# A two-layer hybrid trunk: the loads of the modulation's weights are issued from GpSimd's queue

## The chip, the cores and the metric

The kernel runs on one core of one Trainium2 chip. The metric is the device time of one execution in microseconds (us). The core has five engines with a queue of instructions each: PE (TensorE, the matmuls; PEld is its weight loads), DVE (VectorE), ACT (ScalarE), POOL (GpSimd) and SP (SyncE). Each works through its own queue in order and waits on semaphores for the others. A transfer is issued by an instruction in one engine's queue and carried out by 16 DMA engines.

## The reference, cut to what matters

Two layers of a trunk, each with four groups of heads (latent attention, banded attention, gated delta rule, long convolution) and an MLP, for 128 context and 1024 latent tokens, width 1024, all in float32. The lines that the change touches are those of the modulation:

```python
def trunk_layer(x, cond, P, mixer):
    mod = jnp.einsum('bd,de->be', jax.nn.silu(cond), P['w_ada']) + P['b_ada']
    sh1, sc1, gt1, sh2, sc2, gt2 = jnp.split(mod[:, None, :], 6, axis=-1)
    h = rms_norm(x, P['g_pre_mix']) * (1.0 + sc1) + sh1
    o, extra = mixer(h)
    x = x + gt1 * rms_norm(o, P['g_post_mix'])
    h = rms_norm(x, P['g_pre_mlp']) * (1.0 + sc2) + sh2
    m = jnp.einsum('blf,fd->bld', jnp.square(jax.nn.relu(jnp.einsum('bld,df->blf', h, P['mlp_w1']))), P['mlp_w2'])
    x = x + gt2 * rms_norm(m, P['g_post_mlp'])
```

`w_ada` is 1024 x 6144 in each layer, 24 MB. It depends on nothing but the two conditions (`c` and `c_ctx`), so it may be multiplied long before its result is used.

## The kernel before

All of the kernel is one class, `Trunk`. The modulation is worked out by `ada(l, g)` (line 384), a Python generator, in six groups: layer `l` 0 or 1, and `g` 0 to 2, a third of the columns each (the first two sections, the next two, the last two of the six). One group loads 32 tiles `wada` of 128 x 512 float32 (256 KB; 8 slices `kt` of the contracted width by 4 column blocks `h`) and multiplies each with the conditions into one PSUM tile `ada`; the four matmuls of a `kt` write the four 32-row quarters of it. Then ACT copies the tile out (`adarow`, line 398), PE transposes it (`adat`) and DVE adds the bias (`mod`, line 406).

The tiles `wada` come from the pool of tag `T`, which has four buffers. So a load may be issued only when the matmul that used the buffer four loads earlier is done. Loads of other weights (`wa`, `wb`, `w`) take buffers of the same tag in other stages. Before the change every DMA of the kernel, these loads too, is issued from SP's queue.

`layer(l)` (its caller) runs three generators in turn by a virtual clock, `run_timed((rest(), 1.5), (ahead(other()), GD), (adas(), 1))`. `rest` is the projections, the preparation of the latent attention, the convolution (`hyena`) and the attention; `other` is the delta rule's preparation and scan (`gdn_scan`), at a higher priority; `adas` waits until the projections are done and then steps through `ada` for the groups (l,1), (l,2) and (l+1,0). The group (0,0) runs by itself at the program's start. So in layer 0 three groups (96 loads) run beside the scan, the convolution and the beginning of the attention, and in layer 1 two (64 loads).

The order in which these generators emit is not yet the order of the engines: the program is built under `tile.TileContext(nc, schedule_with_timeline_sim=True)`, whose scheduler orders each engine's instructions by times that it works out for itself. A changed instruction can thus move others on every engine.

Names used below. In `gdn_scan`: `u`, `dS` and `St` are the matmuls and the state of a step, `sc` and `Q` hold its output (lines 1388, 1389), which goes to the DRAM tensor `goscr` (line 1392); after the last step `o` is loaded from `goscr` (line 1413), POOL adds both directions (line 1417), ACT and DVE normalise it and PE transposes it (`oT`). In `hyena`: POOL makes `pm`, `sd` and `ZA` (line 1465) and the two halves of `Y` (lines 1605, 1606); PE transforms (`X`, `iz`). In the attention: `K`, `Q`, `VA` are loaded (lines 752 to 759), `S` are the scores, `mx` their maxima.

Of the kernel before, what the change touches and what calls it, by code (L numbers as in the profile page):

```python
# [158 lines left out]
def bc(ap, n):  # L159

    return ap.unsqueeze(len(ap.shape)).broadcast_to(list(ap.shape) + [n])


class Trunk:
# [220 lines left out]
    def ada(self, l, g, tag="T"):  # L385

        nc = self.nc
        ps = self.P(name="ada")
        for kt in range(8):
            for h in range(4):  # L390
                w = self.H(name="wada", tag=tag[h % len(tag)])
                i = nc.sync.dma_start(out=w, in_=self.I["w_ada"][l, kt, :, g * 2048 + h * 512:g * 2048 + (h + 1) * 512])
                self.mm(ps[32 * h:32 * h + 32, :], self.cst[:, kt], w, kt == 0, kt == 7)
            if l == g == 0:
                self.lead = i
            yield
        row = self.H(name="adarow")
        nc.scalar.copy(out=row, in_=ps)
        pt = self.P((4, 2, 2, 32), name="adat")
        for b in range(4):  # L400
            self.tr(pt[:, b], row[:, b * 128:(b + 1) * 128])

        for half in range(2):
            o = self.mod[l][:, g, half * 4:half * 4 + 4]
            b = self.bada[l].rearrange("p (g s h b) -> p g s h b", g=3, s=2, h=2)[:, g, :, half].rearrange("p s b -> p b s")
            nc.vector.tensor_tensor(out=o, in0=pt[:, :, :, half, 0:2], in1=bc(b, 2), op=ALU.add)
        yield
# [1841 lines left out]
```

## Time and profile before

| | us |
|---|---|
| median of 3 runs | 3819.6 |
| lowest, highest | 3818.95, 3856.05 |
| the profiled execution | 3818.92 |
| its span in the trace | 3817.1 |
| PE busy in the span | 3530.3 |
| DVE busy | 2236.0 |
| ACT busy | 1367.0 |
| POOL busy | 710.1 |

The profile is of one execution. Busy time is what an engine spends in its operations; issues of DMAs, semaphores and branches are not counted in it. A row of the timeline is one group of like instructions in a line: its start, its length, what it did, how many (x), and in brackets how long the engine had been idle before it and what released it. `SPq` is an issue in SP's queue. `DMA` in a window is the mean busy share of the 16 DMA engines, `PEclk` the clock that was granted to PE, 1 being full.

### The profile page before, as it was taken

Reading aid. Unit: us, or ns where it says so; the run is one execution under the profiler, and the core shown is the slowest. Engines: PE = TensorE matmul, PEld = TensorE weight load, DVE = VectorE, ACT = ScalarE, POOL = GpSimd, SP = SyncE. Lnnn points to the kernel's source line nnn. Section 1 sums busy time; section 2 is a strip of 40 time slices with the busy share of each in tenths; the row PEclk is TensorE's granted clock in tenths of the full one; section 3 lists DMA queues with packets and bytes.
Section 4 is the critical chain, followed back from the end, with each engine's and each line's share of the span. In section 5 each row is a group of like instructions: output and inputs, shape, how many; then the busy total and the mean of one; then the engine's idle time right before and its main releaser. Section 6 shows DMA issues by size and latency. Waiting matters only on the chain. (4 is left out here: it accounts for less than half of the span.)

```text
span 3817.1 us, 58820 instructions
## 1 busy us (share of the span) xinstructions
PE 3530.3 (92%) x22478; PEld 2940.8 (77%) x22478; DVE 2236.0 (59%) x4583; ACT 1367.0 (36%) x2972; POOL 710.1 (19%) x710
## 2 busy tenths in 40 slices
PE   7989888799899999999989798787989999999998
PEld 4879774366689999999968787545656899999997
DVE  5765567677645444444586674767774544444446
ACT  5434343265543122212364334323664422222112
POOL 1152531013420000000131633211143200000003
PEclk9998889799999999999999898897989999999999
DMA  5346476832421111111334465755414211111113
GB/s 203 115 115 158 137 266 201 240 84 60 141 86 48 42 45 44 35 44 45 100 104 129 112 151 151 262 185 167 101 40 138 72 45 45 45 45 45 39 39 122
DMA packets 364677, 405.40 MB, mean 106 GB/s; under 512 B 115816, under 2 KB 237158, under 8 KB 364395
## 3 DMA queue, kind: packets, MB, share of 16 engines
q1 hardware_dynamic: 364394, 401.63, 35.1%
q8 instruction: 177, 2.90, 0.3%
q14 instruction: 106, 0.86, 0.1%
HBM read 298.34 MB, written 103.19 MB: 105 GB/s over the span
## 5 line engine op out<-in xcount | busy, mean ns | idle before, releaser
L213 PE MATMUL hid<-hT,w1h 128*128 128x384 f32 x3072 | 786.6, 335 | 0.1
L213 PE MATMUL pj<-hT,wah 128*128 128x384 f32 x2112 | 575.8, 351 | 10.4 <-ACT wah L253 4.2
L1839 DVE TENSOR_TENSOR acc<-acc,mo 128x512 f32<-128x512 f32 x504 | 345.9, 686 | 391.9 <-PE mo L213 391.9
L213 PEld LDWEIGHTS hid<-hT,w1h 128*128 128x128 f32 x3072 | 557.6, 188 | 14.4 <-ACT h L481 1.1
L213 PE MATMUL hid<-hT,w1l 128*128 128x384 f32 x1536 | 514.1, 335 | 0.0
L213 PE MATMUL mo<-w2h,ul 128*128 128x512 f32 x1116 | 435.0, 392 | 0.0
L213 PE MATMUL mo<-w2h,uh 128*128 128x512 f32 x1080 | 422.7, 391 | 0.0
L213 PE MATMUL mo<-w2l,uh 128*128 128x512 f32 x1080 | 422.7, 391 | 0.0
L213 PEld LDWEIGHTS pj<-hT,wah 128*128 128x128 f32 x2112 | 396.3, 196 | 23.3 <-issue 7.5
L213 PE MATMUL pj<-hT,wal 128*128 128x384 f32 x1056 | 368.2, 349 | 0.7 <-DVE wal L232 0.7
L242 ACT CAST w2h<-w 128x512 fp32r<-128x512 f32 x128 | 70.3, 619 | 732.7 <-PE mo L213 728.5
L269 POOL TENSOR_TENSOR postr<-postr,mhalf 128x1 f32<-128x1 f32 x36 | 22.3, 622 | 1564.1 <-DVE postr L268 1563.7
L213 PEld LDWEIGHTS hid<-hT,w1l 128*128 128x128 f32 x1536 | 288.3, 188 | 2.5
L213 PEld LDWEIGHTS mo<-w2h,ul 128*128 128x128 f32 x1116 | 209.6, 188 | 46.1
L662 POOL TENSOR_TENSOR e<-e,e 128x512 f32<-128x512 f32 (+1 forms) x120 | 162.2, 1353 | 445.3 <-ACT e L651 267.4
L213 PEld LDWEIGHTS mo<-w2h,uh 128*128 128x128 f32 x1080 | 202.8, 188 | 37.5
L213 PEld LDWEIGHTS mo<-w2l,uh 128*128 128x128 f32 x1080 | 202.7, 188 | 36.5
L232 DVE TENSOR_TENSOR el<-e,eh 128x512 fp32r<-128x512 f32 (+1 forms) x252 | 202.3, 820 | 32.2 <-ACT eh L653 30.3
L213 PEld LDWEIGHTS pj<-hT,wal 128*128 128x128 f32 x1056 | 206.4, 195 | 4.6 <-issue 2.0
L1822 DVE SCALAR_TENSOR_TENSOR relu<-hid,relu 128x384 f32<-128x384 f32 x180 | 99.4, 553 | 167.2 <-ACT relu L1821 167.2
L213 PE MATMUL ada<-wada,cst 128*32 128x512 f32 x384 | 137.0, 688 | 46.9 <-DMA wada<-in_w_ada 46.7
L1821 ACT ACTIVATE relu<-hid 128x384 f32<-128x384 f32 x180 | 87.8, 488 | 184.8 <-PE hid L213 184.8
(502 smaller groups left out, 6318.1 us busy)
## 6 DMA issues: line engine op xcount, KB each, us to landing
w<-in_w SPq DMA_DIRECT2D x256, 256.0 KB
wada<-in_w_ada SPq DMA_DIRECT2D x192, 256.0 KB
wa<-in_wa SPq DMA_DIRECT2D x88, 256.0 KB
x<-xres SPq DMA_DIRECT2D x21, 512.0 KB
x<-in_x SPq DMA_DIRECT2D x18, 512.0 KB
Q<-rscr SPq DMA_DIRECT2D x32, 288.0 KB
o<-oscr SPq DMA_DIRECT2D x18, 512.0 KB
xres<-x SPq DMA_DIRECT2D x36, 256.0 KB
```

Of the source, the lines that this page charges most:

```text
L213: self.last = self.nc.tensor.matmul(out, l, r, start=start, stop=stop, skip_group_check=True)
L232: self.nc.vector.tensor_tensor(out=lo, in0=x, in1=hi.bitcast(F32), op=ALU.subtract)
L242: self.nc.scalar.copy(out=hi[:, q], in_=st)
L269: self.nc.gpsimd.tensor_tensor(out=out, in0=out, in1=self.bcs(self.mhalf[:out.shape[0]], out.shape), op=ALU.pow)
L662: self.nc.gpsimd.tensor_tensor(out=acc, in0=acc, in1=e, op=ALU.add)
L1821: nc.scalar.activation(out=r[:, :n], in_=ps[:, :n], func=AF.Relu)
L1822: nc.vector.scalar_tensor_tensor(out=r[:, :n], in0=ps[:, :n], scalar=0.0, in1=r[:, :n], op0=ALU.max, op1=ALU.mult)
L1839: nc.vector.tensor_tensor(out=acc[t][:, ns], in0=acc[t][:, ns], in1=ps, op=ALU.add)
```

## The change

One line of `ada`: all loads but those of the group (0,0) are issued from GpSimd's (POOL's) queue. The order of `T`'s buffers, the transfers and the matmuls stay the same in number.

```diff
@@ ada
         for kt in range(8):
             for h in range(4):
                 w = self.H(name="wada", tag=tag[h % len(tag)])
-                i = nc.sync.dma_start(out=w, in_=self.I["w_ada"][l, kt, :, g * 2048 + h * 512:g * 2048 + (h + 1) * 512])
+                i = (nc.gpsimd if g or l else nc.sync).dma_start(out=w, in_=self.I["w_ada"][l, kt, :, g * 2048 + h * 512:g * 2048 + (h + 1) * 512])
                 self.mm(ps[32 * h:32 * h + 32, :], self.cst[:, kt], w, kt == 0, kt == 7)
```

SP's order has 1566 rows before and 1400 now (like rows in a line are joined), POOL's 701 and 861.

The order of the engines at three places. First POOL in layer 0, at the beginning of the convolution's transforms, before:

```order
L535 TENSOR_TENSOR rsh_6277<-rsh_6277,rS_6276 128x512
L1465 TENSOR_TENSOR pm_6473<-v_6296,v_6298 128x512
L1465 TENSOR_TENSOR sd_6474<-v_6296,v_6298 128x512
L1465 TENSOR_TENSOR ZA_6476<-pm_6473,sd_6474 128x512
L1605 TENSOR_TENSOR Y_6601<-pw_6597 128x256
L1606 TENSOR_TENSOR Y_6601<-pw_6597 128x256
L1605 TENSOR_TENSOR Y_6601<-pw_6609 128x256
L1606 TENSOR_TENSOR Y_6601<-pw_6609 128x256
```

and now:

```order
L392 DMA wada_6402<-in_w_ada 128x512
L535 TENSOR_TENSOR rsh_6277<-rsh_6277,rS_6276 128x512
L1465 TENSOR_TENSOR pm_6473<-v_6296,v_6298 128x512
L1465 TENSOR_TENSOR sd_6474<-v_6296,v_6298 128x512
L1465 TENSOR_TENSOR ZA_6476<-pm_6473,sd_6474 128x512
L1605 TENSOR_TENSOR Y_6601<-pw_6597 128x256
L392 DMA wada_6502<-in_w_ada 128x512
L392 DMA wada_6505<-in_w_ada 128x512
L392 DMA wada_6508<-in_w_ada 128x512
L1606 TENSOR_TENSOR Y_6601<-pw_6597 128x256
L1605 TENSOR_TENSOR Y_6601<-pw_6609 128x256
```

Loads of `wada` now stand between `rsh` (the rope of the attention) and `pm`, and between the two halves of the first `Y`.

Then PE in layer 1 after the last step of the scan, before:

```order
L213 MATMUL ada_24334<-wada_24700,cst 32x512
L213 MATMUL ada_24334<-wada_24703,cst 32x512
L213 MATMUL ada_24334<-wada_24706,cst 32x512
L213 MATMUL ada_24334<-wada_24709,cst 32x512
L229 MATMUL oT_24318<-ident,o_24287 128x128 x4
L229 MATMUL oT_24324<-ident,o_24287 128x128 x4
L229 MATMUL oT_24330<-ident,o_24287 128x128
L229 MATMUL adat_24714<-ident,adarow_24712 128x128 x4
L213 MATMUL S_24727<-K_24629,Q_24627 128x384
L213 MATMUL S_24730<-K_24629,Q_24627 128x384
```

and now:

```order
L213 MATMUL ada_24334<-wada_24700,cst 32x512
L213 MATMUL ada_24334<-wada_24703,cst 32x512
L213 MATMUL ada_24334<-wada_24706,cst 32x512
L213 MATMUL ada_24334<-wada_24709,cst 32x512
L229 MATMUL adat_24714<-ident,adarow_24712 128x128 x4
L213 MATMUL S_24727<-K_24629,Q_24627 128x384
L213 MATMUL S_24730<-K_24629,Q_24627 128x384
L213 MATMUL S_24733<-K_24629,Q_24627 128x384
L213 MATMUL S_24733<-Q_24627 128x128
L213 MATMUL S_24737<-K_24629,Q_24627 128x384
```

The transposes `oT` of the scan's output no longer stand between the last `ada` and `adat`; the scores `S` follow in a run.

At the same place SP's order before, four loads of `wada` stood behind the last `goscr` and the loads of `o`, `Q` and `VA`, and four more behind `x`, `gzl`, `K` and `Q`. Now `K`, `Q` and `VA` for the first scores stand ahead of the last `goscr`, and loads of the output projection's weights (`wo`) between those of `o`.

Last PE in layer 1 earlier in the scan, between its sixth and its seventh step of 18 (`pj` are matmuls of the projections), before:

```order
L213 MATMUL dS_22819<-u_22814,sc_22362 64x64 x2
L213 MATMUL dS_22819<-u_22814,kt_22213 64x64 x2
L213 MATMUL dS_22825<-u_22814,sc_22362 64x64 x2
L213 MATMUL dS_22825<-u_22814,kt_22215 64x64 x2
L213 MATMUL pj_23218<-hT_11158,wah_23208 128x384
L213 MATMUL pj_23218<-hT_11157,wal_23210 128x384
L213 MATMUL pj_23218<-hT_11159,wah_23208 128x384
L213 MATMUL pj_23218<-hT_11160,wah_23208 128x384
L213 MATMUL pj_23218<-hT_11159,wal_23210 128x384
L213 MATMUL pj_23218<-hT_11161,wah_23208 128x384
```

and now:

```order
L213 MATMUL u_22797<-u_22814,Q_20957 64x64
L213 MATMUL u_22797<-u_22814,Q_20974 64x64
L213 MATMUL dS_22825<-u_22814,sc_22362 64x64 x2
L213 MATMUL dS_22825<-u_22814,kt_22215 64x64 x2
L213 MATMUL u_22977<-St_3909_22219,sc_22725 64x64
L213 MATMUL u_22978<-St_3909_22219,sc_22725 64x64
L213 MATMUL u_22977<-St_3909_22219,sc_22725 64x64
L213 MATMUL u_22978<-St_3909_22219,sc_22725 64x64
L213 MATMUL u_22977<-St_3909_22219,WT_21834 64x64
```

Before, 19 `pj` matmuls of 128 x 384 stood between the two steps, and more inside the next. Now the seventh step follows the sixth at once; the fifth to the eighth follow each other with little or nothing of other work between, and the `pj` matmuls stand elsewhere.

## Rows read from the trace of the kernel before

**Rows 1.** Page, part 1: busy us, share of the span, instructions of each engine.

```profile
PE 3530.3 (92%) x22478; PEld 2940.8 (77%) x22478; DVE 2236.0 (59%) x4583; ACT 1367.0 (36%) x2972; POOL 710.1 (19%) x710
```

**Rows 2.** Windows: length, busy us (count) PE PEld DVE ACT POOL, PEclk, DMA, GB/s.

```profile
538.00:768.00 230.00, 187.12 (x1440) 100.62 (x1438) 158.40 (x460) 65.30 (x200) 39.05 (x40) 0.87 0.77 239
...
2454.00:2598.00 144.00, 110.10 (x916) 57.11 (x916) 94.74 (x304) 36.75 (x124) 29.82 (x33) 0.89 0.67 213
```

**Rows 3.** Windows of 40 us, the same columns.

```profile
540.00:580.00 40.00, 26.83 (x301) 17.87 (x298) 34.25 (x106) 14.13 (x48) 16.16 (x18) 0.81 0.93 324
...
700.00:740.00 40.00, 29.60 (x136) 14.77 (x135) 22.36 (x57) 10.89 (x19) 2.62 (x1) 0.76 0.98 285
```

**Rows 4.** PE's waits, 538 to 768 us: waiting line, releaser; total us, times, longest.

```profile
PE ada L213 <- DMA wada<-in_w_ada: 15.0, 12, 4.2
PE X L213 <- DVE ZA L1461: 10.7, 2, 8.8
```

**Rows 5.** PE's waits, 2454 to 2598 us.

```profile
PE ada L213 <- DMA wada<-in_w_ada: 30.8, 8, 14.6
```

**Rows 6.** PE's timeline, 2565 to 2604: start, us, operation, count, idle before.

```profile
2565.60 1.06 PE L213 MATMUL ada<-wada,cst 128*32 128x512 f32 x8
...
2567.12 0.45 PE L213 MATMUL u<-u,Q 64*64 64x64 f32 x8
2582.17 4.00 PE L213 MATMUL ada<-wada,cst 128*32 128x512 f32 x8 [14.60 <-DMA wada<-in_w_ada]
2593.82 3.78 PE L213 MATMUL ada<-wada,cst 128*32 128x512 f32 x8 [7.65 <-DMA wada<-in_w_ada]
...
2598.92 0.77 PE L213 MATMUL S<-K,Q 96*128 96x384 f32 x3
...
2602.34 1.53 PE L213 MATMUL S<-K,Q 96*128 96x384 f32 x3 [2.59 <-DVE of L277]
```

**Rows 7.** SP's timeline (issues), 2573 to 2590.

```profile
2573.20 0.42 SPq L759 DMA_DIRECT2D VA<-vascr  x1
2573.67 4.68 SPq L392 DMA_DIRECT2D wada<-in_w_ada  x4
...
2584.11 5.07 SPq L392 DMA_DIRECT2D wada<-in_w_ada  x4
```

**Rows 8.** PE's timeline, 706 to 718.

```profile
706.90 1.94 PE L213 MATMUL ada<-wada,cst 128*32 128x512 f32 x8
...
715.36 1.91 PE L213 MATMUL ada<-wada,cst 128*32 128x512 f32 x2 [4.19 <-DMA wada<-in_w_ada]
```

**Rows 9.** SP's timeline, 712.

```profile
711.94 1.82 SPq L392 DMA_DIRECT2D wada<-in_w_ada  x4
```

**Rows 10.** Line 392: ns min/median/max of one issue; 538:768 and 2454:2600.

```profile
L392 SPq DMA_DIRECT2D wada<-in_w_ada x92: 327/374/992, 551.2 to 761.6; - x92
...
L392 SPq DMA_DIRECT2D wada<-in_w_ada x56: 327/372/1257, 2455.9 to 2588.9; - x56
```

**Rows 11.** POOL's groups over the span: count, busy us, mean ns, idle before.

```profile
L1605 POOL TENSOR_TENSOR Y<-pw 128x256 f32<-128x256 f32 x28 | 20.4, 728 | 62.3 <-DVE pw L1599 61.9 <-POOL Y L1606 0.4
...
L1285 POOL TENSOR_TENSOR vb<-vtok,beta 128x1152 f32<-128x1152 f32 x8 | 18.7, 2342 | 61.1 <-PE G L213 29.2 <-ACT UV L1294 16.7 <-DMA kscr<-kk 15.2
```

**Rows 12.** DVE's timeline, 2591.

```profile
2591.22 1.36 DVE L1430 TENSOR_TENSOR o<-o,of 128x1152 f32<-128x1152 f32 x1
```

**Rows 13.** PE's timeline, 664 to 670: one step of layer 0's scan.

```profile
664.16 0.28 PE L213 MATMUL u<-St,sc 64*64 64x64 f32 x3 [0.25 <-DVE St L1376]
...
665.29 0.33 PE L213 MATMUL u<-u,sc 64*64 64x64 f32 x4 [0.45 <-DVE u L1370]
...
666.18 0.33 PE L213 MATMUL u<-u,sc 64*64 64x64 f32 x4 [0.44 <-DVE u L1370]
...
669.36 0.48 PE L213 MATMUL dS<-u,sc 64*64 64x64 f32 x4 [2.20 <-DVE Q L1389]
```

**Rows 14.** PE's timeline, 2440: layer 1's scan.

```profile
2440.33 0.51 PE L213 MATMUL dS<-u,sc 64*64 64x64 f32 x6 [5.58 <-DVE Q L1389]
```

## The prediction

> **What bounds the kernel now.** I read the busy shares first: PE is busy for 92% of the span [rows 1], so only the 8% in which it waits can be won, and any gain has to be a wait of PE that ends on a load of the modulation's weights (`wada`). Next come the stretches in which these loads run. Four of the 160 that move start before 538 us; 92 are issued between 538 and 768 us (layer 0), 56 between 2454 and 2600 us (layer 1), and the other eight just ahead of that. In both stretches PE is busy for about four fifths, DVE for two thirds, POOL for a sixth to a fifth, and the 16 DMA engines for 0.77 and 0.67 of the time [rows 2]. So no engine is full: what counts are latencies and the order in which queues are served. In single slices, though, the DMA engines are nearly full, 0.93 and 0.98 [rows 3].
>
> PE's waits in the two stretches: 15.0 us for `wada` in layer 0, in 12 pieces of at most 4.2 [rows 4]; 30.8 us in layer 1, in 8 pieces, one of them 14.6 [rows 5]. Together 45.8 us, 1.2% of the time. That is all that could be won on these waits.
>
> The timelines say where. At the end of layer 1's scan eight `ada` matmuls end at 2566.66, which frees the four buffers of tag T, and PE goes on until 2567.57. Then it idles 14.60 us, works 4 us, idles 7.65 us, and the scores `S` start at 2598.92 with 2.59 us more of waiting inside [rows 6]. SP's timeline says why: the loads could have been issued from 2566.6 on, but in SP's order the scan's `goscr` and `o` and the loads of `Q` and `VA` stand ahead, and SP issues them at 2573.67, behind `VA`; the next four go out at 2584.11 [rows 7]. From issue to PE's start it takes 8.5 us (2573.67 to 2582.17). In layer 0 the longest piece is 4.19 us [rows 8]; there the buffers of the eight matmuls before it are free at 708.8 and SP issues at 711.94, 3.4 us before the matmul [rows 9].
>
> **The change part by part.** It moves 160 issues from SP to POOL. No load, matmul or byte is added or gone. The scheduler then orders every engine anew, as the excerpts of the order show.
>
> *Issue.* On SP one costs 0.33 us at least, 0.37 in the median of both stretches, up to 1.26 [rows 10]. What one costs on POOL no row shows, since POOL issues none. Bounds: below, SP's 0.33 us, as the issue is the same request; above, POOL's 128x1152 operations, 2.34 us, the nearest long row of that engine [rows 11]. I take 1.2 us, that of SP where four stand in a row behind busy DMA engines (4.68 us for four [rows 7]). At 1.2 us POOL spends 92 x 1.2 = 110 us in layer 0's stretch and 56 x 1.2 = 67 in layer 1's, beside 39 and 30 of its own work, in 230 and 144 us [rows 2]: it fits. It no longer fits from (230 - 39) / 92 = 2.08 and (144 - 30) / 56 = 2.04 us on.
>
> The cheap issue on SP is hidden behind what SP waits for anyway, so SP's 160 x 0.37 = 59 us are worth nothing by themselves. That `K`, `Q` and `o` loads no longer stand behind `wada` is worth little too: they wait on the scan.
>
> *The tail of layer 1.* Buffers free at 2566.6; four issues at 1.2 us, each landing 3.4 us later (the span of the layer-0 case [rows 8, 9]), the last at 2566.6 + 4.8 + 3.4 = 2574.8; the other four, each as its buffer comes free, 4.8 us later, 2579.6. So `S` may start at about 2580.5 instead of 2598.92: 18 us won. The order helps: `adat` and a run of `S` stand right behind the last `ada`, and `oT`, which waits for a chain on DVE that ends at 2592.6 [rows 12], is put behind them. POOL's `o` addition now stands behind the last `wada` issue, at 2576 to 2580 where it ran at 2578.09: at most 2 us late, covered by that run of `S`.
>
> *The rest of layer 1, and layer 0.* 30.8 - 22.3 = 8.5 us of small pieces and 15.0 us in layer 0. Where SP stood, POOL is free; where the transfer itself is late, nothing changes. The 4.19 us piece splits like that, 3.1 us of SP's delay and 3.4 of transfer. I take half of each: 4 + 7.5 us.
>
> *What it costs.* (1) In the new order four steps of layer 1's scan follow each other with little or none of the projections' matmuls between. A step without filler shows in layer 0: PE waits 0.25 + 0.45 + 0.44 + 2.20 = 3.3 us [rows 13]. Four of them: 13 us. Nothing is won back where the filler went, if PE did not idle there. The bounds are 0 (the filler closes other gaps) and 4 x 5.6 = 22, by the worst single wait of such a step in layer 1 [rows 14]. (2) Issues now stand in front of `Y` and between its halves. A `Y` half is 0.73 us [rows 11], and three issues between halves are 3.6 us. PE already waits 10.7 us for `ZA` [rows 4]. I take 4 us in all.
>
> The sum: 18 + 4 + 7.5 = 29.5 won, 13 + 4 = 17 lost, 12.5 net. The profiled execution took 3818.92 us, 0.7 below the median of 3819.6. 3818.9 - 12.5 = 3806 us.
>
> What the rule of the skill would do to the sum stands by itself. The Trainium skill ("DMA: Bandwidth & Descriptors", Issuing engines are not separate DMA queues) says that a DMA started from another engine runs on the same 16 DMA engines, and that only the sequencer's issue time is saved. By that the result would be that of the third rival below. The issue of four in 4.68 us and the 8.5 us to the landing [rows 6, 7] leave open whether transfer or queue holds it.
>
> **The rivals.**
> - *POOL's issue is the bound (the other side).* If an issue takes the 2.34 us of the upper bound, POOL needs 148 x 2.34 + 69 = 415 us in 374 us: 41 us more, with nothing won and the scan's 13 us lost, 3873 us. Slower by 1% (38 us) begins at (38 - 13 + 374 - 69) / 148 = 2.2 us for one issue. For it: the 128x1152 rows, and DVE busy for two thirds of both stretches [rows 2], with which POOL may share a path. Against it: an issue touches no 128x1152 tile. Chance 0.16. The Trainium skill ("SBUF — State Buffer", the box on "DVE blocks DMA") has a mechanism of this kind: descriptors of a load issued from GpSimd are written by its cores, and they are locked out of SBUF while VectorE runs a copy-like two-port operation. No run so far shows it, as all loads are on SP.
> - *POOL's own work pays.* POOL works in order; a `wada` that waits for its buffer holds `Y` and `ZA` behind it, and the waits for loads become waits for `Y`. If each of the 28 `Y` pairs [rows 11] is late by one issue of 1.2 us, that is 34 us against 29.5 won, and 13 lost: 3818.9 + 17.5 = 3836 us. For it: the order puts issues between `Y` halves, and X waited 10.7 us on this chain. Against it: POOL has more than half of the stretch free. Chance 0.18.
> - *The loads are late by transfer, not by queue.* Slices with 0.93 and 0.98 [rows 3] say it. Nothing is won; the scan's loss, partly covered by the waits that stay, is about 6 us: 3825 us. Against it: in the tail SP issued 7 us after the buffers were free. Chance 0.20.
> - *All of it is won.* 45.8 + 2.6 us of waits gone and no loss: 3770 us. Against it: the transfer of 3.4 us stays, and the order has the bare scan steps. Chance 0.12.
>
> **How the numbers follow.** The forecast has 0.34: 3806 us, its own range 3790 to 3820 (the bounds of the scan's loss, 0 and 22, and of the halves taken). A measurement of this kernel can tell about 1%, 38 us, from no change. Faster by more than that (below 3781) is most of the last rival: 0.11. Slower by more (above 3858) is the first one and a little of the second: 0.18. Within: 0.71. The range from 3776 to 3852 leaves out the first rival and half of the last, some 2 in 10.
>
> **What would show it.** Right: PE's waits on `wada` fall from 45.8 to about 20 us, the 14.60 and 7.65 us are under 8 together, `S` starts some 18 us earlier after the scan's last step, and layer 1's scan shows more waits on DVE. An issue on POOL reads about 1 us, and POOL is busy or issuing for some two thirds of the stretch. Wrong: PE waits for `wada` longer than before with POOL issuing back to back (first rival); waits on `Y` or `ZA` of tens of us (second); issues early and landings as late as before (third).

## The result, and the profile after

The kernel with the loads on POOL is slower: 3859.3 us in the median (3845.8 to 3871.5, 13 executions) against 3834.5 (3805.8 to 3856.1, 13) for the kernel before, measured together; ratio 1.0084, 95% interval 1.0057 to 1.0111. That is 25 us lost, inside the 1% that the prediction called no change, but on the other side of zero from its 12.5 us of gain and above its range. The profiled execution took 3855.7 us, with a span of 3853.9; that of before had 3817.1.

The page of the changed kernel, part 1 and one group (columns as in [rows 1] and [rows 11]):

```profile
PE 3567.3 (93%) x22478; PEld 2959.1 (77%) x22478; DVE 2230.0 (58%) x4583; ACT 1368.0 (35%) x2972; POOL 800.2 (21%) x870
...
L213 PE MATMUL ada<-wada,cst 128*32 128x512 f32 x384 | 145.3, 663 | 21.7 <-DMA wada<-in_w_ada 21.5
```

PE is busy 3567.3 us where it was 3530.3 [rows 1]. So PE idles as long as before: 3853.9 - 3567.3 = 286.6 us against 3817.1 - 3530.3 = 286.8. The waits on `wada` fell and others took their place, and the same 22,478 matmuls took 37 us longer. Most of the 37 us can be put down to TensorE's clock: by the records of the granted clock PE was busy for 290.5 us at the lower of its two levels, half speed, against 237.6 us before, and half of the 52.9 us more is an estimated 26 us. The other 10 or so are not explained. The new waits stand in PE's waits of the two stretches (columns as in [rows 4]); first 540 to 790 us, then 2454 to 2600:

```profile
PE ada L213 <- DMA wada<-in_w_ada: 11.6, 9, 2.0
PE S L213 <- DVE mx L772: 8.1, 7, 2.3
PE X L213 <- DVE ZA L1461: 6.1, 2, 5.3
PE ST L213 <- DMA Q<-mscr: 5.1, 1, 5.1
```

```profile
PE ada L213 <- DMA wada<-in_w_ada: 8.5, 6, 2.4
...
PE S L213 <- DVE mx L772: 4.2, 5, 1.2
```

`wada` fell from 15.0 and 30.8 us [rows 4, 5] to 11.6 and 8.5, 20.1 together. But PE now waits 8.1 + 4.2 us for the row maxima `mx` of the scores, which the first stretch of before hardly had, and 5.1 us for their way through DRAM (`mscr`). Over the whole span, first the change, then before:

```profile
PE ST L213 <- DMA Q<-mscr: 16.4, 2, 11.3
...
PE S L213 <- DVE mx L772: 13.2, 15, 2.3
```

```profile
PE ST L213 <- DMA Q<-mscr: 2.2, 1, 2.2
...
PE S L213 <- DVE mx L772: 0.8, 3, 0.4
```

These two took 26.6 us more, where `wada` took 25.2 less (46.7 before, 21.5 after).

The line of the change, seen from POOL (ns of one issue least, median, most; what POOL waited for ahead of it; us to the landing):

```profile
L392 POOL DMA_DIRECT2D wada<-in_w_ada x160: 536/546/730, 467.8 to 2576.7; - x160
...
  PE ada L213: 169.6, 68
...
DMA to landing us min/median/max: 2.8/3.6/10.3
```

An issue takes POOL 0.55 us, and 0.73 at most. POOL stood 169.6 us, in 68 waits, before an issue until PE gave a buffer back.

The end of layer 1's scan on PE, the place of [rows 6]:

```profile
2577.70 1.05 PE L213 MATMUL ada<-wada,cst 128*32 128x512 f32 x2 [0.96 <-DMA wada<-in_w_ada]
2581.12 3.38 PE L213 MATMUL ada<-wada,cst 128*32 128x512 f32 x6 [2.38 <-DMA wada<-in_w_ada]
...
2585.60 1.10 PE L213 MATMUL S<-K,Q 96*128 96x384 f32 x3
...
2606.07 0.27 PE L229 MATMUL mT<-ident,nm 128*8 128x128 f32 x1
2608.85 2.02 PE L229 MATMUL oT<-ident,o 128*128 128x128 f32 x9 [2.50 <-DVE o L1430]
2613.54 2.18 PE L229 MATMUL oT<-ident,Q 128*128 128x128 f32 x9 [2.67 <-DVE Q L1430]
...
2628.37 1.62 PE L213 MATMUL ST<-Q,K 97*128 97x512 f32 x3 [11.34 <-DMA Q<-mscr]
```

The waits of 14.60 and 7.65 us are gone, and `S` starts at 2585.60 instead of 2598.92 [rows 6]. But the second pass over the scores, `ST`, starts at 2628.37. Before, it started at 2629.05, after a wait of 2.20. It needs the maxima of the first pass as a row of `Q`, and they go `mT`, ACT, a DMA to `mscr`, a DMA back. SP's queue there:

```profile
2612.07 1.53 SPq L2037 DMA_DIRECT2D oscr<-osk  x3
...
2616.92 0.29 SPq L733 DMA_DIRECT2D mscr<-mrow  x1
...
2623.96 0.53 SPq L1440 DMA_DIRECT2D oscr<-gzl  x1
2624.53 0.29 SPq L779 DMA_DIRECT2D Q<-mscr  x1
```

And before, PE and SP:

```profile
2629.05 1.62 PE L213 MATMUL ST<-Q,K 97*128 97x512 f32 x3 [2.20 <-DMA Q<-mscr]
```

```profile
2625.05 0.29 SPq L733 DMA_DIRECT2D mscr<-mrow  x1
...
2627.43 0.24 SPq L779 DMA_DIRECT2D Q<-mscr  x1
```

The maxima were there on ACT at 2607.0 (before, at 2623.9), but the write went out at 2616.92, behind `oscr<-osk` and loads of `K` and `Q`, and the read at 2624.53, behind `oscr<-gzl`. The gain of the tail ends in this wait.

The third difference is TensorE's clock. Windows (columns as in [rows 2]) of the changed kernel, then of the kernel before, two at about the same places and, last, the work of the change's second window (matched as in the table below):

```profile
2604.00:2652.00 48.00, 31.19 (x152) 22.39 (x151) 25.34 (x56) 16.03 (x30) 4.53 (x3) 0.70 0.47 132
...
2804.00:2852.00 48.00, 47.67 (x147) 32.88 (x146) 26.01 (x56) 20.18 (x44) 13.93 (x12) 0.51 0.08 22
```

```profile
2602.00:2645.00 43.00, 38.53 (x161) 26.37 (x162) 32.12 (x66) 11.37 (x21) 0.00 (x0) 0.72 0.62 181
...
2780.00:2828.00 48.00, 45.73 (x260) 28.46 (x258) 38.82 (x85) 29.30 (x62) 19.40 (x15) 1.00 0.08 22
...
2791.60:2821.20 29.60, 29.05 (x145) 19.18 (x145) 25.28 (x58) 19.70 (x44) 15.01 (x12) 1.00 0.13 35
```

In the first window of each the clock is nearly the same. Between 2804 and 2852 us PE is busy for 47.67 of 48.00 us, at a granted clock of 0.51: nearly all of it at the lower level of 1.2 GHz. It does 147 matmuls in 48 us, where the kernel before did 260 in 48 at full clock. The work of these 48.0 us took 29.6 before.

Where the time came from is seen by comparing the two traces at equal work. PE's matmuls are the same in both, so a place in one can be matched with the place in the other at which as much matmul work (counted with the typical time of each shape) is done. The table gives how far each trace is behind the first trace of before, at places of that trace; it also has the experiments, and is read as a sum only where the order around the place is the same. With another choice of the typical time the columns from 2560 to 2740 us move by up to 8 us in single rows, the others by about 1.

```
us of the trace of before     800   1020   2080   2560   2602   2640   2740   2960
the change                   11.9    9.7    9.4    0.7  -10.7    5.0    8.1   34.5
e1 its order, SP             10.0    8.2    8.1    0.3   -9.2    7.9    9.8   46.4
e2 order before, POOL        13.4   13.6   12.2   14.4   15.2   14.8   15.0   36.9
e3 the change again           9.2    7.5    7.1   -1.2  -11.9    3.0    5.3   31.9
e4 only layer 1              -2.3   -1.0   -1.3    1.8   -5.4    6.2    7.3   23.2
e5 maxima early              10.1    8.4    8.2   -1.1  -11.4   -7.0   -4.1   36.9
e6 order before, by times    12.1   32.8   31.3   31.3   31.1   30.3   30.3   32.0
e7 last eight                -1.5   22.4   21.1   19.2   13.7   24.7   29.7   34.9
e8 last eight, maxima         2.8   27.7   27.8   13.6    5.5   12.5   20.9   24.8
e9 before again              -4.8   14.9   14.1   10.2    9.6    9.9    9.9    9.6
e10 only layer 0             17.5   17.2   16.4    6.0    1.5    5.6    9.5   30.1
```

For the change: 11.9 us lost in layer 0 by 800 us; 20.1 won in layer 1 from 2080 to 2602, 8.7 of it before the scan ends (2560) and 11.4 in its tail (by other typical times 3 to 10 and 10 to 17); 15.7 lost again by 2640, at the waits just shown, and 3.1 more by 2740; 26.4 more lost between 2740 and 2960, where the clock is low. A second trace of before (e9) is 4.8 us ahead of the first at 800, so that a few us in the table belong to the execution.

### The profile page after: what moved, and what is told of

It reads as the page before. It is cut to its first block, busy times and chain, and to the rows that moved or that the text cites. A ratio compares the mean times of both kernels' runs of the same rounds, so it can differ in the third digit from the quotient of the medians.

```text
span 3853.9 us, 58897 instructions
## 1 busy us (share of the span) xinstructions
PE 3567.3 (93%) x22478; PEld 2959.1 (77%) x22478; DVE 2230.0 (58%) x4583; ACT 1368.0 (35%) x2972; POOL 800.2 (21%) x870
## 5 line engine op out<-in xcount | busy, mean ns | idle before, releaser
L213 PE MATMUL pj<-hT,wah 128*128 128x384 f32 x2112 | 577.0, 351 | 11.4 <-ACT hc L519 5.0
L213 PE MATMUL ada<-wada,cst 128*32 128x512 f32 x384 | 145.3, 663 | 21.7 <-DMA wada<-in_w_ada 21.5
L232 DVE TENSOR_TENSOR wal<-wa,wah 128x512 fp32r<-128x512 f32 x88 | 63.6, 727 | 174.3 <-ACT wah L253 126.0
```

The source lines that it names most:

```text
L213: self.last = self.nc.tensor.matmul(out, l, r, start=start, stop=stop, skip_group_check=True)
L232: self.nc.vector.tensor_tensor(out=lo, in0=x, in1=hi.bitcast(F32), op=ALU.subtract)
```

## The experiments

Two theories were to be told apart at first. *The queue*: POOL holds the loads or its own work back. *The order*: the scheduler puts all engines in another order when the loads change their engine, and that order is worse. For this the order of one build was written into the other: `ORDER` is the list of places at which a build's engines issue, and each instruction is made to follow the one ahead of it on its engine, without a wait.

```python
for k in order:                       # order = ORDER of the other build
    i = traced[k]; e = str(i.engine)
    if e in last:
        tc.add_manual_dep(i, last[e], DependencyInfo(DependencyClass.NoSync, ...))
    last[e] = i.name
```

**e1: the order of the change, loads on SP.**

```diff
-                i = (nc.gpsimd if g or l else nc.sync).dma_start(out=w, ...)
+                i = nc.sync.dma_start(out=w, ...)        # pinned to the changed kernel's ORDER
```

> The loads stay on SP's queue, but every engine issues in the order that the scheduler made for the changed kernel (each load stands in SP's queue where POOL had it in that order of dispatch). Theory 1, the loss is made by the new order of the engines and not by the queue: slower than before by 1 to 2%, at least as slow as the changed kernel (3855 to 3900 us where before is 3835), with a long stretch of half clock in the attention of layer 1 as in the changed kernel. Theory 2, the loss is made by issuing on POOL: within 0.4% of before.

Ratio to before 1.0084 (1.0054 to 1.0115), 3862.9 us in the median of 6. This is a little less than the 1 to 2% that was expected of the order. PE's waits, the stretch of layer 0 (540 to 790 us) and what follows the tail of layer 1 (2592 to 2700):

```profile
PE ada L213 <- DMA wada<-in_w_ada: 16.1, 7, 5.6
PE S L213 <- DVE mx L772: 8.3, 8, 2.3
...
PE ST L213 <- DMA Q<-mscr: 3.9, 1, 3.9
```

```profile
PE ST L213 <- DMA Q<-mscr: 11.1, 1, 11.1
PE S L213 <- DVE mx L772: 2.9, 5, 1.1
```

With no load on POOL the loss is the whole of the change's, and its table row runs like the change's to 2740: behind in layer 0, ahead at 2602, and the same wait for `mscr` of 11 us. The loads' waits fell nearly as far, too: 27.2 us over the whole span, against 46.7 before and 21.5 after. So of the 25.2 us of `wada` waits that the change removed, the order removes 19.5 and the queue 5.7 (by e2 below, which takes the two the other way round, 24.4 and 0.8).

The order of before pinned with the loads on SP was not run, so that the pinning's own cost is not measured by itself. From 1020 to 2080 us, where no load was moved, the pinned e1, e2 and e6 lose nothing in the table (8.2 to 8.1, 13.6 to 12.2, 32.8 to 31.3).

**e2: the order of before, loads on POOL** (in POOL's queue where the scheduler of before had them go out).

```diff
-                i = nc.sync.dma_start(out=w, ...)
+                i = (nc.gpsimd if g or l else nc.sync).dma_start(out=w, ...)   # pinned to before's ORDER
```

> The 160 loads are issued on POOL's queue, but every engine issues in the order of the kernel before (each load stands in POOL's queue where SP had it in the order of dispatch). Theory 1: faster than before by 5 to 20 us (0.1 to 0.5%), since PE's waits for wada fall from 46.7 to about 20 us and nothing else moves; the wait of 11.3 us for the row maxima (ST on Q<-mscr) stays at about 2 us, and the half-clock time between 2600 and 2960 us at some 45 us. Theory 2: slower by about 0.8%, as the changed kernel.

Ratio 1.0053 (1.0027 to 1.0079), 12 executions: neither the gain that theory 1 expected nor the 0.8% of theory 2. POOL's timeline:

```profile
562.46 0.55 POOL L392 DMA_DIRECT2D wada<-in_w_ada  x1 [9.97 <-PE ada L213]
563.03 0.74 POOL L1605 TENSOR_TENSOR Y<-pw 128x256 f32<-128x256 f32 x1
...
626.78 1.26 POOL L1465 TENSOR_TENSOR pm<-y,y 128x512 f32<-128x512 f32 x1
...
2584.58 2.61 POOL L1417 TENSOR_TENSOR Q<-Q,Q 128x1152 f32<-128x1152 f32 x1 [14.57 <-DVE Q L1389]
2587.13 1.64 POOL L392 DMA_DIRECT2D wada<-in_w_ada  x3
```

So the queue alone loses as well, and through POOL's order of work, in both directions. A load that waits 9.97 us for its buffer holds `Y`; loads ahead of `pm` hold it to 626.78 us, where before it ran at 618.33; and in the tail the loads stand behind an addition that waits 14.57 us for the scan, so that PE waits 11.0 us for them. The trace is 13.4 us behind at 800 us and stays there to 2740. The waits on `wada` are 45.9 us over the span, as before (46.7). Both theories hold: order and queue cost each by itself.

**e3: the change again**, with no edit, beside e1, e2 and e4.

> The changed kernel once more, for a second trace. If the half clock of layer 1's attention belongs to the order, its time at half clock between 2592 and 2955 us is again above 90 us (119.8 in the first trace, 44.4 in before's); if it was a matter of that one execution, it lies near before's. Time 0.5 to 1.1% above before.

Ratio 1.0104 (1.0068 to 1.0139), 4 executions; the same course in the table. The loss repeats, and 1.0084 and 1.0104 show how far two measurements of one kernel stand apart. PE's time at the lower clock between 2592 and 2955 us is 110 us, as expected above 90. But e2, in the order of before, has 118 in the same window, and before itself 49 and, as e9, 59: the order alone does not decide it.

**e4: only layer 1's 64 loads on POOL.**

```diff
-                i = (nc.gpsimd if g or l else nc.sync).dma_start(out=w, ...)
+                i = (nc.gpsimd if l and g else nc.sync).dma_start(out=w, ...)
```

> Only the 64 loads of layer 1 (groups (1,1) and (1,2)) are issued on POOL; the scheduler orders anew. In the first traces layer 0 lost 9.7 us and layer 1 24.8, so if each layer's loss belongs to its own loads: 0.4 to 0.9% slower than before, all of it after 2560 us. If layer 1's loss came from the shift that layer 0 handed on: within 0.3% of before.

Ratio 1.0108 (1.0067 to 1.0150), 4 executions. Layer 0 is as before (-2.3 us at 800), so its loss belongs to its own 96 loads. Layer 1's tail wins 7.2 us by 2602 and loses 11.6 by 2640, 9.0 of it in one wait:

```profile
PE ST L213 <- DMA Q<-mscr: 9.0, 1, 9.0
PE S L213 <- DVE mx L772: 4.0, 4, 3.1
```

**e5: the change, with layer 1's maxima early in SP's queue.** Two entries of the changed kernel's order are moved: the write of `mscr` (L733) and its read (L779) go up in SP's queue, past 12 and 18 other issues by the trace.

```diff
 K<-krowd  Q<-krowd
+mscr<-mrow
 K<-kscr  Q<-kscr  K<-krscr
+Q<-mscr
 Q<-krscr  Q<-qscr  oscr<-osk x3  Q<-qrscr  oscr<-osk  VA<-vascr  oscr<-osk
-mscr<-mrow
 K<-kscr  oscr<-osk  vE<-vascr x2  Q<-kscr  K<-krscr  Q<-krscr  Q<-qscr  oscr<-gzl
-Q<-mscr
 Q<-qrscr  K<-krowd
```

> The changed kernel, every engine in its order, but on SP in layer 1 the write of the first head's row maxima (mscr<-mrow) and their reading back (Q<-mscr) stand 13 and 20 places earlier. Theory A, the 18 us won at the scan's end were lost again in the wait for the row maxima: PE's wait of 11.3 us (ST on Q<-mscr) falls below 2 us and ST starts 9 to 12 us earlier; the time falls by 9 to 12 us against the changed kernel, and if the half clock that follows comes from that wait, by another 10 to 15 us (half clock between 2592 and 2955 us near 70 us and not 90 to 120): 0.2 to 0.5% above before. If the wait is not what counts: as the changed kernel, 0.8 to 1.0% above before.

SP's timeline, and PE's:

```profile
2608.49 0.26 SPq L733 DMA_DIRECT2D mscr<-mrow  x1
2610.62 0.22 SPq L779 DMA_DIRECT2D Q<-mscr  x1
```

```profile
2615.92 1.48 PE L213 MATMUL ST<-Q,K 97*128 97x512 f32 x3
```

`ST` starts at 2615.92 with no wait ahead of it, 12.5 us earlier, and the trace keeps the tail's gain (-7.0 at 2640, -4.1 at 2740). So the wait was SP's order. The rest was lost in this trace where the clock was low: 0.51 for 38 us from 2748 on and 0.50 for 58 from 2806. That the time at the lower clock would fall with the wait was a miss: it is 149 us between 2592 and 2955. Over 12 executions the ratio is 1.0057 (1.0031 to 1.0082), 0.27 and 0.47% under the two measurements of the change, but with intervals that overlap theirs.

**e6: as e2, with the loads placed in POOL's queue by the times at which SP issued them in the trace of before**, so that none stands ahead of work that could go earlier.

```diff
-POOL: ORDER of e2 (loads at the scheduler's own times)
+POOL: ORDER with loads and work merged by their times in the trace of before
```

> As e2_order_before_queue_pool (every other engine in the order of before, the 160 loads on POOL), but the loads stand in POOL's queue where the measured times of before's trace put them among POOL's own work, not where the scheduler's own times put them. Theory B, e2 lost because loads that wait for a buffer held POOL's pm, ZA and Y behind them (pm in layer 0 at 626.8 us, 618.3 before; one load waited 9.97 us ahead of Y): pm is back within 3 us of before's place, X's waits for ZA do not grow, and the time is within 0.2% of before. If instead a load on POOL costs by itself (its issue of 0.55 us, its landing of 4.0 us): 0.4 to 0.6% above before, as e2.

Ratio 1.0032 (1.0005 to 1.0059). That `pm` would be back at its place was a miss: it ran at 628.90 us, since the buffers now came free later than in the trace of before and POOL waited 6.18, 5.31 and 4.81 us for PE. The tail is clean (nothing lost or won from 2080 to 2740), the 12.1 us of layer 0 stay. An in-order queue that is laid out by another run's times does not get those times back.

**e7: only the last eight loads on POOL**, those of the 14.60 and 7.65 us.

```diff
-                i = nc.sync.dma_start(out=w, ...)
+                i = (nc.gpsimd if l and g == 2 and kt >= 6 else nc.sync).dma_start(out=w, ...)
```

> Only the last eight loads (group (1,2), kt 6 and 7) go to POOL; up to the end of layer 1's scan all engines stand as before. The tail by itself: PE's waits of 14.6 and 7.65 us for wada fall to under 6 together, S starts about 13 us earlier. By theory A these come back as a wait of 8 to 12 us of ST on Q<-mscr: without what the clock does, 0 to 5 us faster than before; with half clock after it, up to 0.5% slower. By the prediction's own sum, 18 us (0.5%) faster.

Ratio 1.0053 (1.0021 to 1.0086). The tail wins 5.5 us by 2602 and loses 11.0 by 2640 and 5 more by 2740: a wait for `mscr` of 8.4 us, 4.38 in one wait for `mx`, and the clock:

```profile
2589.00:2633.00 44.00, 30.27 (x74) 15.49 (x75) 33.34 (x85) 4.65 (x8) 7.36 (x6) 0.50 0.93 249
```

PE is busy for 30.27 us of that stretch, so that the clock may account for up to 15 us of the loss, and how much of it is the wait's cannot be told from this trace. The eight loads that carried 18 of the 29.5 us that the forecast booked as won show no gain even alone.

**e8: e7, and the write and read of `mscr` on POOL too.**

```diff
-        nc.sync.dma_start(out=self.mscr[l, j, ...], in_=r[:n]...)
+        nc.gpsimd.dma_start(out=self.mscr[l, j, ...], in_=r[:n]...)
-        self.row = nc.sync.dma_start(out=Q[0][96:97, 0:1024]..., in_=self.mscr[l, h:h + 1, 0:1024])
+        self.row = nc.gpsimd.dma_start(out=Q[0][96:97, 0:1024]..., in_=self.mscr[l, h:h + 1, 0:1024])
```

> As e7_last_eight_on_pool, and the row maxima of the latent attention's heads are written and read back through POOL's queue too, so that SP's loads do not stand ahead of them (the scheduler orders anew from layer 0's attention on). Theory A: the wait of ST on Q<-mscr is 3 us or less in both layers and the tail's gain stays: 8 to 15 us faster than before (0.2 to 0.4%). If the order decides alone, it may lie anywhere within 1% of before.

Ratio 1.0024 (0.9996 to 1.0052): no difference from before, and not the 8 to 15 us of gain that were expected. Of the wait of `ST` for `Q<-mscr` 0.3 us are left; PE's waits from 2592 to 2700 us are now

```profile
PE S L213 <- DVE mx L772: 6.5, 6, 3.6
PE oT L229 <- DVE o L1430: 5.0, 1, 5.0
PE hoT L229 <- ACT osk L2036: 4.1, 1, 4.1
```

15.6 us on DVE's and ACT's chains. Each queue that is cleared shows the next engine that has not yet done its part. This was the fastest of the versions that moved loads, and it doesn't beat the kernel before; how much of its lead over e7 is the clock's is estimated behind e10. (Its trace has a low-clock step in layer 0, and layer 1 in another order.)

**e9: the kernel before again.** More than half of the change's 34.5 us stood between 2740 and 2960, most of it in one stretch at low clock, and the question was whether the change causes it.

> The kernel before, unchanged, for a second trace of it and for the size of a difference that is none. If the long stretches at half clock are a matter of the execution and not of the order of the work, this trace has its time at half clock somewhere between 370 us (the first trace of before) and 460 us (the last eight loads alone on POOL), and its span is longer than 3817 us by about 0.4 us for each us at half clock above 370. If they belong to the moved loads, there is no stretch of more than 30 us at half clock, as in the first trace of before. The ratio to the kernel before should be 1.000 within 0.003 either way.

Ratio 0.9996 (0.9969 to 1.0023). Its trace has a span of 3826.6 us, and in it the first of these windows; the second has the same work (matched as in the table) in the first trace of before:

```profile
907.00:955.00 48.00, 48.00 (x142) 31.38 (x141) 23.03 (x52) 18.78 (x40) 13.61 (x12) 0.51 0.08 22
```

```profile
911.70:939.90 28.20, 27.80 (x141) 18.32 (x140) 24.18 (x53) 18.41 (x40) 14.57 (x12) 1.00 0.14 37
```

Here it is in the very same program: 48 us at a clock of 0.51, in the banded attention of layer 0, which costs 20 us (48.0 against 28.2, and -4.8 to 14.9 in the table). So a stretch of this kind does not need the change. The span is 9.6 us longer than the first, not the 22 that 0.4 us for each of its 54 us more at the lower level (424 against 369) would make: between two single traces that rule is rough. In the table every trace has one step of 16 to 41 us, either between 800 and 1020 (e6 to e9) or between 2740 and 2960 (the change, e1 to e5, e10), where the banded attention of layer 0 or of layer 1 runs; in e4, where it is smallest, without one long stretch at low clock. Only the first trace of before, against which all are held, has neither. It was a fortunate execution: 3818.9 us, where the medians of before in three later comparisons were 3826.6, 3830.8 and 3836.3.

**e10: only layer 0's 96 loads on POOL.**

```diff
-                i = (nc.gpsimd if g or l else nc.sync).dma_start(out=w, ...)
+                i = (nc.gpsimd if (l == 0) == (g > 0) else nc.sync).dma_start(out=w, ...)
```

> The 96 loads of the groups (0,1), (0,2) and (1,0) on POOL, those of layer 1's stretch on SP. On PE the order is that of the changed kernel up to layer 1, and nearly that of before from there on. If layer 0's new order makes its own part of the loss (the 8 to 10 us by which the changed kernel is behind at 800 us of the span): ratio 1.002 to 1.003, and the same 8 to 10 us at that place, where the kernel with only layer 1's loads moved had none. If the loss in layer 0 is given back by idle time behind it: ratio 1.000. If the two layers' parts add up, this one and the one with layer 1's loads alone (1.0108) cannot both be as large as the whole change (1.0084 to 1.0104): above 1.005 here would speak against a sum.

Ratio 1.0059 (1.0036 to 1.0082), above the 1.002 to 1.003 that its own part was given. The trace is 17.5 us behind at 800 us, more than the change. The scheduler orders layer 1 anew too, though no load of it moved, and PE's waits for `wada` in layer 1's stretch are

```profile
PE ada L213 <- DMA wada<-in_w_ada: 5.4, 5, 2.3
```

5.4 us with these loads on SP, where the kernel before had 30.8: once more the order, not the queue. The two layers' parts don't add up (0.6 + 1.1% against 0.8 to 1.0%), as each comes with an order of its own for the rest.

What of the loss is clock, and what is not, can be estimated over all executions. Among 35 of before, the time grows by 0.37 us for each us at the lower level, and by 0.29 to 0.47 in the others, but for the eight of e10, which show no such growth (time at the lower level: the share that the mean granted clock lacks, doubled, as one level is half of the other). Before lies at 400 to 408 us of it in the mean of each comparison, the change at 426 and, as e3, at 443: 18 to 43 us more, or 7 to 16 us of time at 0.37. So of the 27 and 37 us lost in the mean, an estimated 21 remain at equal clock (17 to 25 with the slopes of 0.47 and 0.29). The traces place only a part of them: ahead of the stretch at low clock, at 2740 us, the change is 8.1 us behind and e3 5.3, and where the rest lies is open. That the mean low time is larger in the change's order (e1 430, e5 436, e10 432) is measured; why the clock falls there more often is not settled. By the same estimate some 5 us remain of e7's 24 us in the mean (460 us at the lower level) and 13 of e8's 8 (394 us), so that at equal clock the maxima's DMAs on POOL are not shown to gain anything.

## Why the prediction was wrong, step by step

**The loads' waits: right in size.** From 45.8 to about 20 us was expected; 20.1 was measured, and of the 14.60 + 7.65 us in the tail 2.38 + 0.96 stayed ("under 8 together"). `S` was to start at 2580.5 and did at 2585.60, 13.3 us earlier instead of 18. That the size came out is partly luck: the forecast took SP's queue as what holds the loads, and e1, with them on SP in the new order, has most of the gain.

**POOL's issue: sized too high, without effect.** 1.2 us was taken between 0.33 and 2.34; it is 0.55, and 0.73 at most. The first rival needed 2.2 and falls. In this trace, with DVE busy for 58% of the span, no issue was held. The Trainium skill ("SBUF — State Buffer", the box on "DVE blocks DMA") describes a lock-out of GpSimd's descriptor writes while VectorE runs a two-port operation such as a float32 copy; no run here shows one, with 536 to 730 ns for 160 issues, and none shows whether such an operation ran beside them.

**The tail's 18 us: the step that failed.** The prediction booked them as won because `adat` and a run of `S` stand behind the last load, and asked no further what is late next. The gain was there (11.4 us at 2602). But behind the run of `S` comes `ST`, which needs the maxima of all of them. They were ready 16.4 us earlier (`mT` at 2606.07 against 2622.51) and then lay: their write and read stood behind other transfers in SP's queue, so that `ST` waited 11.34 us, and `oT` ahead of it 2.50 and 2.67 us for the scan's normalising. `ST` starts at 2628.37 against 2629.05, and by 2640 more is lost than was won: 18 us booked, 11.4 - 15.7 = -4.3 measured. e5 shows that SP's order is the wait; e7 has the same wait (8.4 us) with eight loads alone, and in e8 DVE and ACT come last. A row of before pointed there: `ST` already waited 2.20 us for `mscr` behind its `S`, so its place in SP's queue, and not the start of `S` alone, set when it could go on.

**The small pieces, 7.5 and 4 us.** In layer 0 3.4 us of waits went (15.0 to 11.6), in layer 1 outside the tail 3.3 (30.8 - 22.3 = 8.5, now 8.5 - 3.3 = 5.2): 6.7 of the 11.5 booked.

**The bare scan steps, 13 us lost: not seen.** From 2080 to 2560 the change won 8.7 us, e1, e3 and e5 as much (7.8 to 9.3; by other typical times less, but nothing is lost). PE's waits at the scan's matmuls (`u`, `dS`) are 15.9 us from 2080 to 2575, where they were 19.8: steps without filler wait (4.5 us once), but others wait less, as the lower bound of 0 said.

**`Y` behind issues, 4 us: wrong place.** PE's wait for `ZA` fell from 10.7 to 6.1 us in layer 0 (8.4 over the span, with layer 1's). Layer 0 lost 11.9 us in another way: the new order mixes the scores into the scan's end, PE waits 8.1 us for `mx`, and the maxima are stuck again. ACT's copy of the row stands behind one that waits for `oscr`, then SP's read follows late:

```profile
721.64 0.75 ACT L2036 COPY osk<-hoT 128x512 f32<-128x512 f32 x2 [8.14 <-DMA oscr<-osk]
722.28 0.25 ACT L732 CAST mrow<-mT 8x128 fp32r<-8x128 f32 x1
```

```profile
734.73 1.62 PE L213 MATMUL ST<-Q,K 97*128 97x512 f32 x3 [5.06 <-DMA Q<-mscr]
```

Before, `ST` ran at 728.67. No run moves layer 0's maxima by themselves, as e5 does layer 1's, so that this part is read from the trace and not tested. The second rival ("POOL's own work pays") named a real mechanism, and e2 shows it at three places, but in the change's own order POOL's 169.6 us of waiting for buffers cost PE little: its wait for `ZA` fell. Its loss of 17.5 us (3836 us) was the nearest to the 25 us measured, and for the most part for another reason; that the measured 3859 us lies nearer to the first rival's 3873 is chance, as the issue took 0.55 us.

**The sum by places, to 2740 us.** Layer 0 (with the 4 us for `Y`): 7.5 - 4 = 3.5 us won were booked, 11.9 lost were measured (2.5 came back by 2080). Layer 1 up to 2602: 18 + 4 - 13 = 9 booked, 20.1 measured. From 2602 to 2740: nothing booked, 18.8 lost. So 12.5 us won became 8.1 lost, by the new waits in layer 0 and above all by those behind the tail, which no term of the sum held; e5, without the wait for `mscr`, loses 7.3 there.

**The third rival** said that the queue is not what holds the loads. On this the runs are clear: with the loads on SP but in the new order, 27.2 us of waits are left (e1), with them on POOL in the old order 45.9 (e2). That agrees with the Trainium skill ("DMA: Bandwidth & Descriptors", Issuing engines are not separate DMA queues): changing the engine alone bought 5.7 us of waits in the new order and 0.8 in the old. The rest came from the order.

**The baseline and the clock: a term that was missing.** The sum was made against one execution of 3818.9 us, and its three timed ones had a median of 3819.6; in four comparisons before had medians of 3826.6 to 3836.3. So 8 to 17 us of the miss of 53 (3859.3 - 3806) are the baseline's, and in the comparison of the result itself 15.6 (3834.5 - 3818.9). A term for the clock, an estimated 7 to 16 us, was not in the sum at all, though the three runs' spread of 37 us said that something of this size varies.

## What to carry to other kernels

Before a wait's end is booked as time, follow the work behind it to the next thing that does not move, here a chain of maxima that goes through two DMAs at the end of another queue; what is won ahead of it is only a longer wait there. Changing a DMA's engine in a kernel that a scheduler orders can change the order of every engine, and here that order was the larger part of the effect: pin the order to see what the queue itself is worth. When one program's executions spread over 1%, take the baseline from many of them, and look in the trace whether the profiled one has the stretches at low clock that most have.

## What the runs showed of the hardware

- A stretch of some 48 us at the lower clock can come or stay away in the same program and place: the 142 matmuls of 48.0 us in one execution of before took 28.2 us in another. PE is fully busy in it (48.00 of 48.00 us) and the DMA engines nearly idle (0.08).
- Over 35 executions of one program the time grew by 0.37 us for each us at the lower level, less than the half that a PE without waits would lose.
- A DMA of 256 KB costs POOL 0.55 us of issue where SP took 0.33 at least and 0.37 in the median [rows 10], with little scatter (0.73 at most against 1.26 on SP). It landed 3.6 us after its issue in the median (2.8 to 10.3).
